# RWKV on one NeuronCore: zeros behind the first norms, an order edge on the scaling of y, and gate stores from another queue

## The chip, the core and the metric

The kernel runs on one core of a Trainium2 chip. The metric is the device time of one execution in microseconds (us). The kernel before took 1004.63 us, the median of three runs (1004.32 to 1005.11). A core has a matrix engine, TensorE (PE; its weight loads are listed as PEld), three engines for element-wise work, VectorE (DVE), ScalarE (ACT) and GpSimd (POOL), and SyncE (SP), which here only issues DMA transfers. ACT and POOL can issue transfers too. Each engine works through its own list of instructions in order, and waits for the others by semaphores.

## The reference

One layer of a hybrid decoder on 512 prompt tokens and 8 x 8 sampled tokens (576 columns in all), all in float32. RWKV-7 time mixing and a paged differential attention read the same normalised input; sigmoid gates mix their outputs; then comes an MLP. The parts that matter here:

```python
def rwkv7_scan(S0, r, w, k, v, a, b):
    def step(S, inp):
        r_t, w_t, k_t, v_t, a_t, b_t = inp
        sa = jnp.einsum('bhij,bhj->bhi', S, a_t)
        S = S * w_t[:, :, None, :] + sa[..., None] * b_t[:, :, None, :] + v_t[..., None] * k_t[:, :, None, :]
        return S, jnp.einsum('bhij,bhj->bhi', S, r_t)
    S, ys = lax.scan(step, S0.astype(jnp.float32), xs)

def rwkv7_branch(Pr, S0, lp):
    ...
    kk = kk / jnp.maximum(jnp.linalg.norm(kk, axis=-1, keepdims=True), 1e-12)
    ...
    S, y = rwkv7_scan(S0, hs(r), hs(decay), hs(k), hs(v), -kk, kk * hs(a))
    mean = jnp.mean(y, axis=-1, keepdims=True)
    var = jnp.mean(jnp.square(y - mean), axis=-1, keepdims=True)
    y = (y - mean) * lax.rsqrt(var + GN_EPS) * lp['ln_x_w'] ... + lp['ln_x_b'] ...
    ...

def layer_forward(x, prev_row, S0, attend, lam_init, lp):
    ...
    gate_a = jax.nn.sigmoid(P[..., off2:off2 + D_MODEL])
    gate_b = jax.nn.sigmoid(P[..., off2 + D_MODEL:off2 + 2 * D_MODEL])
    m = gate_a * (o_a @ lp['w_br_a']) + gate_b * (o_b @ lp['w_br_b'])
```

## The kernel before

Activations lie with channels on the 128 partitions and the 576 tokens along the free axis. A product with a weight matrix is a *stream*: weights are loaded as `raw` tiles by SP, split into a rounded part `hi` (ACT) and a rest `lo` (DVE), and PE runs three matmuls for each block of weights (`xh,hi`, `xl,hi`, `xh,lo`) over two halves of the columns. The result lands in a bank (`ps_g`, `ps_z`), from which DVE evacuates it.

The eight heads of RWKV are worked on as four pairs of heads, `hp` 0 to 3, and these two at a time (`pr` 0 and 1). For each `hp` the generator `rwkv(hp)` runs in stages:

- The first stage (lines 751 to 840) makes the norms of k: `sq`, its sums `pn` on PE, `nr` on DVE, the power -0.5 on POOL (L760), and `nb`, the norm spread out over 64 columns, by a copy on POOL (L763). PE transposes `nb` to `pk` and `pks`, and DVE multiplies k by them (`sq` again, the unit key). Decays come by a scan on DVE (`cum`) and exponentials on ACT (`pe`, `pinv`, `u`). Then DVE writes the tiles KB and ST, PE multiplies them (`pA`), and DVE evacuates them to ABR and ST. One half of each ST is cleared by POOL (L818).
- The second stage puts v into SVU (transposes `pV`), KB into KBt (`pK`), and loads the sampled sequences' state `s0` (L859, SP). `pI` on PE multiplies ST and that state. POOL copies an identity into SVU (L871) and clears a part of it (L872).
- The third inverts the 32x32 blocks (`pW`, `pZ`, matmuls of 32x32 tiles) and writes TT; POOL clears two parts of TT (L923, L924).
- The fourth updates the state: `pF` on PE, whose input `vm` comes from POOL; two operations on DVE (`s<-s,pF`, the addition, and `s<-s,pc`, the scaling); and a store by POOL's queue (L941). The tile of `hp` + 2's state uses the buffer of `hp`'s.
- The last ones, behind the recurrence, normalise y over 64 columns: `mean`, the square, `var`, a power on POOL, the scaling `tt(y, y, b9(var), MUL)` on DVE (L958), transposes `pTy`, and the products with the gate of RWKV, `pg`.

`chain(pr)` is the recurrence over nine chunks of 64 tokens: small matmuls `pch` and `pY` (64x64 tiles), each waiting for a copy on ACT or DVE. Between them the scheduler puts the gate matmuls: `gate(g)` for 16 blocks of output channels streams w_in (`ps_g`), scales each half (`gg`, DVE), applies tanh (ACT), and stores the result in `gt_d` in device memory (L452), from where it is read back at the merge.

What stands where on each engine is set by the scheduler: it takes the program's order, the priorities that `prio` sets, and order edges, `tc.issue_after(x)`, which keep an instruction behind instruction x in the list. `ring["mm"]` is the last matmul or transpose so far, `take(n)` lets the streams that are waiting advance by n steps.

Of the kernel before, what the change touches and what calls it, by code (L numbers as in the profile page):

```python
# [15 lines left out]
P = 128  # L16
# [20 lines left out]
C_ID, C_OB, C_M, C_MS, C_LM, C_I32, C_HS, C_SEL, C_MB, C_CM, C_END = (  # L37
    0, 128, 256, 384, 512, 672, 704, 706, 738, 746, 748)
# [3 lines left out]
def tile_hybrid_step(ctx, tc, xT, xsT, ktab, vtab, s0T, ptab, w_in, vecs, w2a2, g2, lamv,  # L42
                     w_bra, w_brb, w_out, w_up, w_down, cst, bias_p, bias_s,
                     yT, kTo, vTo, Sp, Ss, sh):
    nc = tc.nc
    PE, VE, AE, GE = nc.tensor, nc.vector, nc.scalar, nc.gpsimd
# [8 lines left out]
    ring = {"job": 0}  # L55

    def act(out, in_, func=AF.Copy, **kw):
        ring["act"] = AE.activation(out=out, in_=in_, func=func, **kw)  # L58

    def tt(out, a, b, op, eng=None):  # L60
        ins = (eng or VE).tensor_tensor(out=out, in0=a, in1=b, op=op)  # L61
        if eng is None:
            ring["tt"] = ins

    def stt(out, a, s, b, op0, op1):
        VE.scalar_tensor_tensor(out=out, in0=a, scalar=s, in1=b, op0=op0, op1=op1)
# [4 lines left out]
    def mm(out, lhsT, rhs, start=True, stop=True):  # L71
        ring["mm"] = PE.matmul(out=out, lhsT=lhsT, rhs=rhs, start=start, stop=stop)  # L72
        return ring["mm"]
# [17 lines left out]
    MUL, ADD, SUB, MAX = ALU.mult, ALU.add, ALU.subtract, ALU.max  # L91
# [12 lines left out]
    def tbank(name):  # L104
        return psc.tile([P, 512], F32, tag="t", name=name)
# [6 lines left out]
    c = const.tile([P, C_END], F32, name="cst_sb")  # L112
# [103 lines left out]
    def take(n):  # L216

        while waiting and n:
            if next(waiting[0], None) is None:
                waiting.pop(0)  # L220
            else:
                n -= 1
# [42 lines left out]
    gt_d = tc.dram_tile([2 * KT, P, NT], F32, name="gt_d")  # L265
# [178 lines left out]
    def gate(g):  # L444

        gg = gs.tile([P, NT], F32, tag="gg", name=f"gg{g}")

        def ev(ps, t0, n):
            tt(gg[:, t0:t0 + n], ps, R1[:, t0:t0 + n], MUL)
            act(gg[:, t0:t0 + n], gg[:, t0:t0 + n], AF.Tanh, scale=0.5)  # L450
        yield from stream(w_in[26 + g], KT, xh, xl, HALF, ev, f"g{g}")
        nc.sync.dma_start(out=gt_d[g], in_=gg)  # L452

    def ob_halves():

# [209 lines left out]
    for h in range(HB):  # L665
        if h:
            qkv(h)
        for cc in range(2):
            GE.tensor_copy(
                out=qbd[64 * cc:64 * cc + 64, :, h, 8 * cc:8 * cc + 8],  # L670
                in_=qT[64 * cc:64 * cc + 64, h, NPR:].rearrange("p (b q) -> p b q", b=NB))
# [47 lines left out]
    def ch(a):  # L719
        return a.rearrange("p (c t) -> p c t", t=64)  # L720

    def m3(ap_, n):
        q, w = ap_.shape
        return ap_.rearrange("p (o w) -> p o w", o=1).broadcast_to([q, n, w])
# [17 lines left out]
    def rwkv(hp):  # L742
# [5 lines left out]
        def tmp(tag, bufs=1):  # L748
            return rt.tile([P, NT], F32, tag="T", name=f"{tag}_{hp}", bufs=6)


        sq = tmp("sq")
        act(sq, k, AF.Square, scale=v(V_KK + hp))
        pn = bank(f"pn{hp}")
        for t, o in enumerate(toks):
            mm(pn[:, 2 * t:2 * t + 2], sq[:, o:o + P], c[:, C_HS:C_HS + 2])
        (fill if hp != 2 else take)(8)
        nr = stat.tile([P, 10], F32, tag="nr", name=f"nr{hp}")
# [1 line left out]
        GE.tensor_tensor(out=nr, in0=nr, in1=mhalf[:, :10], op=ALU.pow)  # L760

        nb = rt.tile([P, 5, P], F32, tag="G", name=f"nb{hp}", bufs=3)
        GE.tensor_copy(out=nb.rearrange("p t (a d) -> p (t a) d", a=2),  # L763
                       in_=nr.rearrange("p (a o) -> p a o", o=1).broadcast_to([P, 10, 64]))
        u = tmp("u")
        aa = tmp("aa")
        for t0, n in HALF:
# [46 lines left out]
        for par, rows in halves:  # L814
            stt(KB[rows, :, par], ch(aa)[rows], 0.5, ch(pinv)[rows], MUL, MUL)
            tt(KB[rows, :, 1 - par], ch(k2)[rows], ch(pinv)[rows], MUL)
            st = rb_.tile([P, NCH, 2, 64], F32, tag=f"ST{par}", name=f"ST{par}_{hp}")
            GE.memset(st[64 - 64 * par:128 - 64 * par], 0.0)  # L818
            stt(st[rows, :, 0], ch(kk)[rows], -1.0, ch(pm)[rows], MUL, MUL)
            tt(st[rows, :, 1], ch(r)[rows], ch(pe)[rows], MUL)  # L820
            ST.append(st)
# [4 lines left out]
        for par in range(2):  # L826
            rows = slice(64 * par, 64 * par + 64)
# [14 lines left out]
        SVU = own["SVU"][:, :, e]  # L842
# [23 lines left out]
        for par in range(2):  # L866
            rows = slice(64 * par, 64 * par + 64)
            for a in range(2):
                act(ST[par][rows, 8, a].rearrange("p (b t) -> p b t", b=NB),
                    pI[rows, 0:P].rearrange("p (b a t) -> p b a t", b=NB, a=2)[:, :, a])  # L870
            GE.tensor_copy(out=SVU[rows, 8, par], in_=c[rows, C_ID + 64 * par:C_ID + 64 * par + 64])  # L871
            GE.memset(SVU[rows, 0, par], 0.0)  # L872

        yield

# [10 lines left out]
        def blocks(ps, lhs, rhs, n):  # L886
            for ci in range(n):
                for g in range(4):
                    gs = slice(32 * g, 32 * g + 32)
                    last = mm(ps[gs, ci * 32:ci * 32 + 32], lhs[gs, ci], rhs[gs, ci])  # L890
            with tc.issue_after(last.ins):
                take(9)
            return ps[:, :n * 32].rearrange("p (c s) -> p c s", c=n)
# [3 lines left out]
        for l in range(1, 5):  # L897

            n = NCH if l < 3 else 8
            DM = rt.tile([P, NCH, 32], F32, tag="DM", name=f"DM{hp}_{l}")  # L900
            tt(DM[:, :n], DT[:, :n], m3(c[:, C_LM + 32 * l:C_LM + 32 * l + 32], n), MUL)
            W = rt.tile([P, NCH, 32], F32, tag="W", name=f"W{hp}_{l}")
            act(W[:, :n], blocks(tbank(f"pW{hp}{l}"), DM, X, n))
            tt(X[:, :n], X[:, :n], blocks(tbank(f"pZ{hp}{l}"), Y, W, n), ADD)
            VE.transpose(out=Y[:, :n], in_=X[:, :n])
        TT = rb_.tile([P, NCH, 64], F32, tag="TT", name=f"TT{hp}")
        pW = tbank(f"pWc{hp}")
# [11 lines left out]
        for b0, b1 in quads:  # L919
            act(TT[b0, :8, 32:64], pC[b0, :256].rearrange("p (c s) -> p c s", c=8))  # L920
            act(TT[b0, :, 0:32], Y[b0])
            act(TT[b1, :, 32:64], Y[b1])
            GE.memset(TT[b0, 8:, 32:64], 0.0)  # L923
            GE.memset(TT[b1, :, 0:32], 0.0)  # L924

        own[e] = ST, KBt, TT, ABR, pc
        yield
# [16 lines left out]
        y = own["y"][:, e]  # L944
# [4 lines left out]
        b9 = lambda a: a.rearrange("p (c o) -> p c o", o=1).broadcast_to([P, NCH, 64])  # L949
# [3 lines left out]
        var = stat.tile([P, NCH], F32, tag="var", name=f"var{hp}")  # L953
# [1 line left out]
        rpow(var, var, 1.0 / 64, 64e-5)  # L955

        yield
        tt(y, y, b9(var), MUL)  # L958
        oa = rt.tile([P, NT], F32, tag="G", bufs=3, name=f"oa{hp}")
        if hp >= 2:  # L960
            half_rows(hp)
# [79 lines left out]


    gens = [rwkv(hp) for hp in range(4)]

    def run(*stages):
        for hp in stages:
            while Pt[8 + hp] is None:
                take(2)
            next(gens[hp], None)

    waiting += zs(2) + zs(3) + [gate(g) for g in range(KT, 2 * KT)]
    ga = [gate(g) for g in range(KT)]
    waiting += ga[:5]
    run(0, 0)
# [33 lines left out]
    for d in range(KT):  # L1088
        g = []
        for i in range(2):  # L1090
            gg = rt.tile([P, NT], F32, tag="T", name=f"g{i}_{d}", bufs=6)
# [32 lines left out]
    for i, d in enumerate((0, 4, 1, 5, 2, 6, 3, 7)):  # L1124
# [31 lines left out]
        for j, (t0, n) in enumerate(HALF):  # L1156
            o = acc[:, t0:t0 + n]
# [142 lines left out]
    rows = []  # L1300
    for d, n in enumerate((None, "t1", "b11", "t2", "b21", "t3", "b22", "t4")):
        if n:
            t = fp.tile([P, 2, 4, 288], F32R, tag=f"h_{n}", name=f"w3_{d}", bufs=1)
            t = t.rearrange("p i k t -> p (i k t)")
# [179 lines left out]
```

## Time and profile before

| | us |
|---|---|
| median of three runs (lowest, highest) | 1004.63 (1004.32, 1005.11) |
| the profiled execution's own time | 1006.88 |
| its span | 1005.1 |
| PE busy in the span | 975.1 (97%) |
| DVE busy | 688.9 (69%) |
| ACT busy | 497.0 (49%) |
| POOL busy | 87.5 (9%) |
| mean granted clock of PE | 0.993 |

The profile is of one execution. The span is from the first to the last instruction that it recorded. Rows of a timeline have the start in us, the duration, the engine, the line of the kernel, the operation, output<-inputs with their shapes, and the number of instructions in the row; in square brackets stand the engine's idle time before and what ended it. A row with several instructions lasts from the start of the first to the end of the last. Matmuls overlap, so that their starts tell how fast PE goes on. `SPq`, `ACTq` and `POOLq` are the queues on which an engine issues transfers. The names in the timeline leave the buffers' numbers out.

### The profile page before, as it was taken

To read this page: it belongs to the slowest core of one execution; us is meant where nothing else is said; L and a number is where in the kernel's file an instruction comes from. 1 tells how busy PE (TensorE), PEld (TensorE's weight loads), DVE (VectorE), ACT (ScalarE), POOL (GpSimd) and SP (SyncE) were. 2 spreads that over 40 slices of the span, in tenths; PEclk is the share of its full clock that TensorE was granted. 3 is DMA by queue.
4 is the path that set the end of the run, shared out by engine and by line. 5 is a ranking of instruction groups with operands and counts; after the bars stand their busy time and mean duration, and the time that the engine had idled before them with its cause. 6 is when DMAs were issued, how large, how long until landed. Compare 5 with 4: busy or idle time off the path is not lost.

```text
span 1005.1 us, 24415 instructions
## 1 busy us (share of the span) xinstructions
PE 975.1 (97%) x10012; PEld 919.4 (91%) x10012; DVE 688.9 (69%) x1459; ACT 497.0 (49%) x1094; POOL 87.5 (9%) x171
## 2 busy tenths in 40 slices
PE   9999999899999998999989999999999999999996
PEld 9999998898887887988779999999999999999996
DVE  6698566864946679444579898966666666666644
ACT  6576455354435355453334666644444444444732
POOL 2511001301010340000210000000000000000001
PEclk9999999999989999999999999999999999999999
DMA  7422673211111234323357642222222222221402
GB/s 266 136 70 83 205 223 114 61 64 45 43 59 45 69 106 152 104 81 113 103 182 225 206 140 86 83 95 85 88 92 85 85 84 85 84 87 41 135 3 95
DMA packets 50833, 105.75 MB, mean 105 GB/s; under 512 B 6066, under 2 KB 8114, under 8 KB 50594
## 3 DMA queue, kind: packets, MB, share of 16 engines
q1 hardware_dynamic: 47442, 96.95, 30.4%
q0 software_dynamic: 1648, 5.35, 1.5%
q8 instruction: 79, 1.29, 0.5%
q10 hardware_dynamic: 1632, 1.89, 0.5%
q14 instruction: 32, 0.26, 0.1%
HBM read 89.38 MB, written 14.78 MB: 104 GB/s over the span
## 4 chain that ended last, share of the span: by engine, by line
PE 83%; DVE 6%; ACT 4%; issue 3%; DMA 2%; POOL 1%; SPq 0%; DVEq 0%; ACTq 0%; POOLq 0%
PE ps_dn L72 20%; PE ps_g L72 8%; PE ps_z L72 8%; PE ua L1220 5%; PE ux L1220 5%; PE ps_wo L72 4%; PE ps_k L72 3%; PE uc L1220 3%; PE ub L1220 3%; PE ud L1220 2%; PE ps_bra L72 2%; PE ps_q L72 2%; PE pch L72 2%; PE ps_brb L72 2%; PE ps_v L72 2%
## 5 line engine op out<-in xcount | busy, mean ns | idle before, releaser
L72 PE MATMUL ps_dn<-q,hi_dn 128*128 128x288 f32 x768 | 154.7, 296 | 0.0
L72 PEld LDWEIGHTS ps_dn<-q,hi_dn 128*128 128x128 f32 x768 | 122.7, 188 | 1.4
L72 PE MATMUL ps_dn<-q,lo_dn 128*128 128x288 f32 x384 | 113.2, 295 | 0.0
L72 PE MATMUL ps_g<-xl,hi_g 128*128 128x288 f32 x256 | 79.7, 311 | 0.0
L72 PE MATMUL ps_g<-xh,hi_g 128*128 128x288 f32 x256 | 79.0, 309 | 0.0
L72 PE MATMUL ps_g<-xh,lo_g 128*128 128x288 f32 x256 | 79.0, 309 | 0.0
L72 PEld LDWEIGHTS ps_dn<-q,lo_dn 128*128 128x128 f32 x384 | 72.0, 188 | 0.0
L72 PE MATMUL ps_z<-xh,lo_z 128*128 128x288 f32 (+1 forms) x224 | 68.9, 308 | 0.0
L72 PE MATMUL ps_z<-xh,hi_z 128*128 128x288 f32 (+1 forms) x224 | 67.6, 302 | 0.0
L72 PE MATMUL ps_z<-xl,hi_z 128*128 128x288 f32 (+1 forms) x224 | 66.8, 298 | 0.0
L61 DVE TENSOR_TENSOR ya<-ya,ps_dn 128x288 f32<-128x288 f32 x96 | 43.2, 451 | 29.4 <-PE ps_dn L72 29.4
L58 ACT ACTIVATE hi_dn<-raw_dn 128x512 fp32r<-128x512 f32 x48 | 30.1, 628 | 57.0 <-PE ps_dn L72 57.0
L1220 PE MATMUL ua<-h_b,hi 128*128 128x288 f32 x256 | 53.2, 298 | 0.0
L1220 PE MATMUL ux<-h_t,hi 128*128 128x288 f32 x256 | 52.3, 296 | 0.0
L58 ACT ACTIVATE c<-c 128x288 f32<-128x288 f32 x112 | 48.4, 439 | 7.4 <-DVE c L61 5.8
L72 PEld LDWEIGHTS ps_g<-xh,hi_g 128*128 128x128 f32 x256 | 48.7, 190 | 3.1 <-issue 1.8
L72 PEld LDWEIGHTS ps_g<-xl,hi_g 128*128 128x128 f32 x256 | 48.6, 190 | 1.9
L72 PEld LDWEIGHTS ps_g<-xh,lo_g 128*128 128x128 f32 x256 | 48.6, 190 | 1.6 <-DVE lo_g L61 0.2
L58 ACT ACTIVATE hi<-a 128x1024 fp32r<-128x1024 f32 (+1 forms) x32 | 27.1, 846 | 42.0 <-PE ps_dn L72 34.2
L72 PE MATMUL ps_dn<-q,w 128*128 128x320 f32 (+1 forms) x336 | 46.3, 297 | 0.0
L61 DVE TENSOR_TENSOR lo<-s,hi 128x1024 fp32r<-128x1024 f32 x32 | 39.2, 1224 | 10.1 <-ACT hi L58 10.0
L72 PEld LDWEIGHTS ps_dn<-q,w 128*128 128x128 f32 x336 | 45.3, 190 | 0.1
(395 smaller groups left out, 2802.2 us busy)
## 6 DMA issues: line engine op xcount, KB each, us to landing
a<-in_w_up_dram SPq DMA_DIRECT2D x32, 512.0 KB, 3.4
raw_dn<-in_w_down_dram SPq DMA_DIRECT2D x64, 256.0 KB, 2.8
raw_g<-in_w_in_dram SPq DMA_DIRECT2D x32, 256.0 KB, 3.1
raw_z<-in_w_in_dram SPq DMA_DIRECT2D x28, 256.0 KB, 3.1
gt_d<-gg SPq DMA_DIRECT2D x16, 288.0 KB, 2.4
g<-gt_d SPq DMA_DIRECT2D x16, 288.0 KB, 3.6
kp<-in_ktab_dram SPq DMA_DIRECT2D x16, 256.0 KB, 4.5
vp<-in_vtab_dram SPq DMA_DIRECT2D x16, 256.0 KB, 3.8
```

Of the source, the lines that this page charges most:

```text
L58: ring["act"] = AE.activation(out=out, in_=in_, func=func, **kw)
L61: ins = (eng or VE).tensor_tensor(out=out, in0=a, in1=b, op=op)
L72: ring["mm"] = PE.matmul(out=out, lhsT=lhsT, rhs=rhs, start=start, stop=stop)
L1220: ring["mm"] = PE.matmul(out=ps[:, :288], lhsT=l[:, k], rhs=hb[blk][:, h, k], start=start and i == 0, stop=i == 11, skip_group_check=skip)
```

## The change

Three edits:

1. `clear(a)` takes the place of POOL's memsets of ST, SVU and TT. For `hp` 0 it keeps the memset behind the copy to `nb` (an order edge); for the others it is the plain memset. The copy of the identity into SVU stands behind `nb` for every `hp`.
2. The scaling of y gets an order edge behind a matmul: for `hp` 0 and 1 behind `ring["mid"]`, which is set at the fourth step of the block inversion of the `hp` that ran it last, and for 2 and 3 behind the last matmul so far.
3. The store of each gate block is issued on ACT's queue and no longer on SP's.

```diff
@@ gate(g)
         yield from stream(w_in[26 + g], KT, xh, xl, HALF, ev, f"g{g}")
-        nc.sync.dma_start(out=gt_d[g], in_=gg)
+        nc.scalar.dma_start(out=gt_d[g], in_=gg)
@@ rwkv(hp)
+        def clear(a):
+            if hp:
+                GE.memset(a, 0.0)
+            else:
+                with tc.issue_after(ring["nb"].ins):
+                    GE.memset(a, 0.0)
...
-        GE.tensor_copy(out=nb.rearrange("p t (a d) -> p (t a) d", a=2),
+        ring["nb"] = GE.tensor_copy(out=nb.rearrange("p t (a d) -> p (t a) d", a=2),
...
-            GE.memset(st[64 - 64 * par:128 - 64 * par], 0.0)
+            clear(st[64 - 64 * par:128 - 64 * par])
...
-            GE.tensor_copy(out=SVU[rows, 8, par], in_=c[rows, C_ID + 64 * par:C_ID + 64 * par + 64])
-            GE.memset(SVU[rows, 0, par], 0.0)
+            with tc.issue_after(ring["nb"].ins):
+                GE.tensor_copy(out=SVU[rows, 8, par], in_=c[rows, C_ID + 64 * par:C_ID + 64 * par + 64])
+            clear(SVU[rows, 0, par])
...
             tt(X[:, :n], X[:, :n], blocks(tbank(f"pZ{hp}{l}"), Y, W, n), ADD)
+            if l == 3:
+                ring["mid"] = ring["mm"]
             VE.transpose(out=Y[:, :n], in_=X[:, :n])
...
-            GE.memset(TT[b0, 8:, 32:64], 0.0)
-            GE.memset(TT[b1, :, 0:32], 0.0)
+            clear(TT[b0, 8:, 32:64])
+            clear(TT[b1, :, 0:32])
...
-        tt(y, y, b9(var), MUL)
+        with tc.issue_after((ring["mid"] if hp < 2 else ring["mm"]).ins):
+            tt(y, y, b9(var), MUL)
```

The first place is POOL's list at the first norms, before:

```order
L711 DMA ob_d<-obs 128x4x64
L818 MEMSET ST_0_2814 64x1152
L818 MEMSET ST_0_2820 64x1152
L760 TENSOR_TENSOR nr_2749<-nr_2749,mhalf 128x10
L871 COPY SVU_2861<-cst_sb 64x64
L872 MEMSET SVU_2861 64x64
L763 COPY nb_2752<-nr_2749 128x640
L871 COPY SVU_2861<-cst_sb 64x64
```

and of the changed kernel:

```order
L712 DMA ob_d<-obs 128x4x64
L755 MEMSET SVU_2861 64x64 x2
L769 TENSOR_TENSOR nr_2749<-nr_2749,mhalf 128x10
L772 COPY nb_2752<-nr_2749 128x640
L758 MEMSET ST_0_2814 64x1152
L758 MEMSET ST_0_2820 64x1152
L881 COPY SVU_2861<-cst_sb 64x64
L758 MEMSET SVU_2861 64x64
```

The memsets of ST and the copies into SVU now stand behind `nb`; two small memsets of SVU, which belong to another `hp`, stand ahead of the power.

The second place is PE's list in the first recurrence, at its second chunk (`pch` and `pY` of that chunk, `ps_g` of a gate, `pk` of `hp` 1), before:

```order
L76 MATMUL pk_4920<-cst_sb,nb_4884 128x128
L72 MATMUL pch_4602<-SVU_2861,ST_0_2814 64x64
L72 MATMUL pch_4602<-SVU_2861,ST_0_2820 64x64
L72 MATMUL pch_4602<-SVU_2861,ST_1_3829 64x64
L72 MATMUL pch_4602<-SVU_2861,ST_1_3835 64x64
L72 MATMUL pY_4603<-SVU_2861,ST_0_2814 64x64
L72 MATMUL pY_4603<-SVU_2861,ST_0_2820 64x64
L72 MATMUL pY_4603<-SVU_2861,ST_1_3829 64x64
L72 MATMUL pY_4603<-SVU_2861,ST_1_3835 64x64
```

and of the changed kernel:

```order
L72 MATMUL pch_4602<-SVU_2861,ST_0_2814 64x64
L72 MATMUL pY_4603<-SVU_2861,ST_0_2814 64x64
L72 MATMUL ps_g_0_4512<-xl,hi_g_1_4508 128x288
L72 MATMUL ps_g_0_4512<-xh,lo_g_1_4509 128x288
L72 MATMUL pch_4602<-SVU_2861,ST_0_2820 64x64
L72 MATMUL pch_4602<-SVU_2861,ST_1_3829 64x64
L72 MATMUL pY_4603<-SVU_2861,ST_0_2820 64x64
L72 MATMUL pY_4603<-SVU_2861,ST_1_3829 64x64
L72 MATMUL pch_4602<-SVU_2861,ST_1_3835 64x64
L72 MATMUL pY_4603<-SVU_2861,ST_1_3835 64x64
```

The eight small matmuls stood together; now two gate matmuls stand between them, and in other places some that stood apart stand together. Over the whole list PE changes between full 128x128 matmuls and small tiles 262 times before and 274 times now.

The third place is DVE's list where the states of `hp` 0 and 1 are finished (`s_0`, `s_1`), before:

```order
L61 TENSOR_TENSOR s_0_2891<-s_0_2891,pF_4992 128x512
L61 TENSOR_TENSOR s_1_3905<-s_1_3905,pF_5002 128x512
L61 TENSOR_TENSOR s_0_2891<-s_0_2891,pc_2782 128x512
L61 TENSOR_TENSOR lo_g_1_5259<-raw_g_4_5252,hi_g_1_5258 128x512
L61 TENSOR_TENSOR s_1_3905<-s_1_3905,pc_3797 128x512
L61 TENSOR_TENSOR gg_5181<-ps_g_1_5195,R_108 128x288
L61 TENSOR_TENSOR lo_g_0_5407<-raw_g_0_5402,hi_g_0_5406 128x512
L61 TENSOR_TENSOR Y_5614<-DT_5609,cst_sb 128x288
```

and of the changed kernel:

```order
L61 TENSOR_TENSOR s_0_2891<-s_0_2891,pF_4992 128x512
L61 TENSOR_TENSOR s_1_3905<-s_1_3905,pF_5002 128x512
L61 TENSOR_TENSOR gg_5181<-ps_g_1_5195,R_108 128x288
L61 TENSOR_TENSOR lo_g_0_5407<-raw_g_0_5402,hi_g_0_5406 128x512
L61 TENSOR_TENSOR s_0_2891<-s_0_2891,pc_2782 128x512
L61 TENSOR_TENSOR s_1_3905<-s_1_3905,pc_3797 128x512
L61 TENSOR_TENSOR Y_5614<-DT_5609,cst_sb 128x288
```

One evacuation of a gate and one split of weights now stand ahead of the scaling. On PE the second `pF` has three gate matmuls between it and the first, where it had six, and 46 instead of 58 gate matmuls lie between the first `pF` and `pI`, with thirty `pW` more.

The list of POOL differs by edit 1, and one memset of ST for `hp` 3 moves as well; those of PE, DVE, ACT and SP by edit 3 alone. With edit 2 alone every list reads as before.

More of the change, by code (lines that the diff above doesn't have):

```diff
@@ L762, in rwkv @@
         nb = rt.tile([P, 5, P], F32, tag="G", name=f"nb{hp}", bufs=3)
-        GE.tensor_copy(out=nb.rearrange("p t (a d) -> p (t a) d", a=2),
-                       in_=nr.rearrange("p (a o) -> p a o", o=1).broadcast_to([P, 10, 64]))
+        ring["nb"] = GE.tensor_copy(out=nb.rearrange("p t (a d) -> p (t a) d", a=2),
+                                    in_=nr.rearrange("p (a o) -> p a o", o=1).broadcast_to([P, 10, 64]))
         u = tmp("u")
```

## The prediction

> **What bounds the kernel now.** I read the head of the page first, then the list of what TensorE (PE) waited for, then timelines of the places that the change touches. The first fence has the span and the busy shares, and from the list of waits the rows that come up below; their columns are total us, times, longest us.
>
> ```profile
> span 1005.1 us, 24415 instructions
> PE 975.1 (97%) x10012; PEld 919.4 (91%) x10012; DVE 688.9 (69%) x1459; ACT 497.0 (49%) x1094; POOL 87.5 (9%) x171
> ...
> PE pk L76 <- POOL nb L763: 2.7, 1, 2.7
> ...
> PE pTy L76 <- DVE y L61: 1.2, 1, 1.2
> ...
> PE pI L72 <- DMA s<-in_s0T_dram: 0.7, 1, 0.7
> ...
> PE pch L72 <- ACT SVU L58: 0.5, 1, 0.5
> ...
> PE pF L72 <- POOL vm L61: 0.3, 1, 0.3
> ```
>
> PE is busy for 975.1 of 1005.1 us, so only 30 us of the span are idle time of PE. A change gains what it takes from those 30 us and loses what it adds to them or to PE's own work. The longest single wait, 2.7 us, is for `nb` in the first norms, where the change begins. SyncE (SP), ScalarE (ACT) and GpSimd (POOL) count only where PE ends up waiting for them.
>
> **The zeros on GpSimd.** The timeline round the first norms, one piece for each of POOL, PE and DVE, with a row that sums a later stretch:
>
> ```profile
> 177.01 2.16 POOL L818 MEMSET ST<- 64x1152 f32 x2
> 179.14 2.18 POOL L760 TENSOR_TENSOR nr<-nr,mhalf 128x10 f32<-128x10 f32 x1
> ...
> 181.47 0.14 POOL L872 MEMSET SVU<- 64x64 f32 x1
> 181.56 0.71 POOL L763 COPY nb<-nr 128x640 f32<-128x640 f32 x1
> ...
> 179.37 0.30 PE L72 MATMUL ps_z<-xh,lo_z 128*128 128x296 f32 x1
> 182.32 0.66 PE L76 MATMUL pk<-cst_sb,nb 128*128 128x128 f32 x4 [2.66 <-POOL nb L763]
> ...
> 175.79 0.16 DVE L69 TENSOR_SCALAR nr<-pn 128x10 f32<-128x10 f32 x1
> ...
> 180.79 0.43 DVE L61 TENSOR_TENSOR Z<-ps_z,R 128x288 f32<-128x288 f32 x1
> 183.02 0.75 DVE L66 SCALAR_TENSOR_TENSOR sq<-P,vec,pk 128x512 f32<-128x512 f32 x1 [1.79 <-PE pk L76]
> ...
> 190.00:200.00 10.00, 9.79 (x72) 9.10 (x70) 9.80 (x17) 1.27 (x2) 0.00 (x0) 1.00 0.21 59
> ```
>
> The input of the power `nr` is there at 175.95 (175.79 + 0.16), but POOL clears the two halves of ST until 179.17 before it starts. In the new order two small clears of SVU (0.14 each) stand in that place; both wait only for things of long before. The power then starts at 177.01 + 0.3 = 177.3 and ends at 179.5, and `nb` follows at once and ends at 180.2 instead of 182.27. PE has nothing else until `pk` and ended its matmul at 179.67, so its wait shrinks from 2.66 to some 0.6 us: -2.1. Who is late next is VectorE (DVE): it is busy with Z until 181.22, so `sq` starts there instead of at 183.02: -1.8. Behind `sq` DVE is busy in 9.80 of the 10 us from 190 on, and PE waits for that work at `pbn`, so I take what DVE gains, **-1.8 us**. The bounds are -2.1 and 0: zero if the later part of that stretch ends on something else than DVE. The clears of ST now come behind `nb` and end at 180.2 + 2.16 = 182.4; what reads ST comes behind the work that DVE only begins with `sq`, so this work hides them. Were they needed at once, PE would lose up to those 2.2 us again.
>
> **The scaling of y.** The new wait names a matmul, and an order edge behind it; the instruction on DVE keeps its neighbours, and no row on any engine moves for this edit alone. It costs and gains **0**. Had it moved the scaling behind more work, PE's 1.2 us wait of `pTy` for y is where it would show.
>
> **The gate stores.** Sixteen DMA issues leave SP's queue and enter ACT's. These are the issues of the stores now, of a store on ACT, and two rows on waiting:
>
> ```profile
> L452 SPq DMA_DIRECT2D gt_d<-gg x16: 319/326/331, 287.7 to 498.5; - x16
> ...
> L1366 ACTq DMA_DIRECT2D out_yT_dram<-ya x4: 378/388/407, 983.2 to 1001.3; - x4
> ...
> SPq L452 <- ACT gg L58: 34.4, 14, 5.3
> ...
> ACT hi_g L58 <- PE ps_g L72: 20.6, 16, 2.8
> ```
>
> On ACT they cost 16 x 0.39 = 6.2 us, on an engine that is busy for 49%. SP is rid of 34.4 us of waiting ahead of the weight loads queued behind a store. But that was not on the path: the split of gate weights on ACT (`hi_g`) waits for PE to let go of a buffer, 16 times, not for a load. So the move itself gives and takes about 0; the upper bound is one issue of 0.39 on the way mean, square, y, `pTy` of the last pair, where a store stands ahead of the square: 0 to +0.4, and I take +0.1.
>
> What does cost is that the order of the other engines changes with it. First, the recurrence (`pch`, `pY`) is cut into smaller groups among the gate matmuls. A stretch of PE's timeline shows the price:
>
> ```profile
> 309.48 0.29 PE L72 MATMUL ps_g<-xl,hi_g 128*128 128x288 f32 x1
> 309.61 0.29 PE L72 MATMUL ps_g<-xh,lo_g 128*128 128x288 f32 x1
> 309.83 0.45 PE L72 MATMUL pch<-SVU,KBt 128*64 128x64 f32 x8
> 310.21 0.45 PE L72 MATMUL pY<-SVU,ABR 64*64 64x64 f32 x8
> 310.59 0.40 PE L72 MATMUL ps_g<-xh,hi_g 128*128 128x288 f32 x1
> 310.83 0.30 PE L72 MATMUL ps_g<-xl,hi_g 128*128 128x288 f32 x1
> ```
>
> Gate matmuls start 0.13 apart (309.48, 309.61); from the last of them to the first small one it is 0.22, and the first gate matmul behind the small ones holds its place for 0.24 before the next. Each switch so costs about 0.1 us. Counted over the two orders PE switches 262 times before and 274 times now: 12 x 0.1 = **+1.2** (bounds 0.5 and 1.5). Against it, a matmul of the recurrence that stands later waits less for ACT and DVE; the list of waits has 0.5 us for `pch` behind SVU as its largest: **-0.4** (bounds -0.9 and 0).
>
> Second, the load of the next pair's state. It overwrites the buffer of the first pair's state, so it waits for that state's store, which waits for two additions and two scalings on DVE. The rows in order of time, the load from the chain of waits, and the landing times of the store (2.4/3.2/4.5) and of the load:
>
> ```profile
> 354.71 0.40 PE L72 MATMUL ps_g<-xh,hi_g 128*128 128x288 f32 x1
> 354.81 0.69 DVE L61 TENSOR_TENSOR s<-s,pF 128x512 f32<-128x512 f32 x1 [0.91 <-PE pF L72]
> 355.42 0.69 DVE L61 TENSOR_TENSOR s<-s,pc 128x512 f32<-128x512 f32 x1
> 356.40 0.57 POOL L941 DMA_DIRECT2D out_Ss_dram<-s  x1 [1.28 <-DVE s L61]
> 357.55 0.45 DVE L61 TENSOR_TENSOR gg<-ps_g,R 128x288 f32<-128x288 f32 x1
> 357.98 0.69 DVE L61 TENSOR_TENSOR lo_g<-raw_g,hi_g 128x512 fp32r<-128x512 f32 x1
> 358.59 0.45 DVE L61 TENSOR_TENSOR Y<-DT,cst_sb 128x288 f32<-128x288 f32 x1
> ...
> 359.44 4.86 DMA s<-in_s0T_dram
> ...
> 364.44 1.11 PE L72 MATMUL pI<-ST,s 64*64 64x16 f32 x32 [0.66 <-DMA s<-in_s0T_dram]
> ...
> DMA to landing us min/median/max: 2.4/3.2/4.5
> ...
> DMA to landing us min/median/max: 3.6/4.0/4.9
> ```
>
> In the new order the evacuation `gg<-ps_g` and the split `lo_g` stand between the additions and the scaling. The evacuation needs the nine gate matmuls behind the second `pF`: they start with the second addition, 9 x 0.13 = 1.2 us. Then come 0.43 (357.55 to 357.98) and 0.61 (to 358.59). The scaling starts at 354.81 + 1.3 + 0.43 + 0.61 = 357.15 instead of 355.42, 1.7 us later, and store and load with it. PE, however, gets to `pI` sooner after `pF`: 12 gate matmuls fewer lie between (-1.6), thirty small `pW` more (+0.6), and the second `pF` has three gate matmuls ahead of it instead of six, so that its wait for `vm` (0.3 now) grows by some 0.4. That makes 0.6 less. The wait at `pI` becomes 0.66 + 1.7 + 0.6 = 3.0 us, or 2.1 if the load lands in its median of 4.0 instead of 4.86. With the 0.4 at `pF` the place costs between 1.9 and 2.7; I take **+2.2**, and keep 0 below (a load that lands in 3.6 behind a store that lands in 2.4, with PE held up elsewhere) and 3.2 above.
>
> **Sum:** -1.8 + 0 + 0.1 + 1.2 - 0.4 + 2.2 = +1.3 us. The profiled execution took 1006.88 us for its span of 1005.1; the median of the runs is 1004.63, 2.25 below it. I carry the difference over: 1008.2 for a profiled execution, **1005.9 us** as a median. A measurement here can tell about 0.2% (2.0 us) from no change, and +1.3 is less.
>
> **Rivals.** *The orders are free and only the zeros count.* The wait at `pI` stays at 0.66, if the store's landing and not DVE's place in line decides, and the switches hide in waits. For it: the load took 4.86 where its median is 4.0. Against it: the store is issued right behind the scaling. Then -1.8 and little else, 1002.8; with the other -0.4, 1002.4.
>
> *A half clock behind the new wait.* These are two windows of the span (length, then busy time of PE, PEld, DVE, ACT and POOL, then the granted clock):
>
> ```profile
> 508.85:512.26 3.41, 1.55 (x8) 1.09 (x9) 1.75 (x4) 1.83 (x6) 1.58 (x1) 1.00 0.76 227
> 512.26:515.68 3.42, 3.42 (x14) 3.20 (x13) 3.10 (x6) 0.42 (x2) 0.22 (x1) 0.50 0.39 115
> ```
>
> After a window of 3.41 us in which PE worked 1.55 us, the next is granted half the clock. A 3 us wait at `pI`, followed by small matmuls, could make such a window. The price is at most half of one window, 1.7 us; since PE also waits there I put 1.5 on top of the sum: 1007.4, slower than before by 2.8. It decides from the point where the wait exceeds about half a window inside one of them. Against it: the 2.66 us wait at 179.67 had full clock behind it. The Trainium skill ("TensorE: Matmul & The Clock Gate", Part 1, "What's actually happening") speaks of a free-running window of 3413 ns and of half clock after a window that was idle. By that rule a wait of 3.0 us, shorter than a window, would cost no clock; the row of 1.55 us of work does not agree with it.
>
> *The zeros' gain is given back.* DVE's early start at 181.2 ends in a wait for ACT's exponentials or for weights before 205, and the rest stands: 0 + 0.1 + 0.8 + 2.2 = +3.1, 1007.7.
>
> **How the numbers follow.** The sum as worked out 0.45, within 1004.0 to 1007.2 by the bounds of its terms; the free orders 0.25; the half clock 0.2; the gain given back 0.1. Faster by over 2.0 us (below 1002.6) happens in some two thirds of the second case and hardly in the first: 0.19. Slower by over 2.0 (above 1006.6) has the half clock, the gain given back and about a tenth of the sum's own case: 0.34. Within: 0.47. The range runs from 1002.5, where the free orders begin, to 1008.6, the half clock with the upper bound at `pI`.
>
> **What would show it.** Right: `pk` waits some 0.6 us for `nb` and `sq` starts 1.8 earlier; the longest wait of PE is then `pI` for the state's load, 2 to 3 us; the gate stores' issues on ACT take 0.39 and SP's list lacks them; the y waits are as before. Wrong: `pI` waits under 1 us, or `pbn` takes up what `pk` lost, or a second window of half clock stands near 366, or PE's work between 285 and 350 has not grown by about 1 us.

## The result and the profile after

The changed kernel takes 1013.95 us, the median of five runs (1011.52 to 1015.28), against 1004.89 us for the kernel before in the same comparison (1004.32 to 1005.94, five runs). The ratio is 1.0079 with a 95% interval of 1.0066 to 1.0092: about 8 us slower by the ratio and 9.1 by the medians, where 1.3 us were forecast and 1008.6 us was the end of the range. (The ratio is worked out from the runs of both kernels and is not the quotient of their medians.) The profiled execution took 1011.52 us, the fastest of the five, and that of the kernel before, 1006.88, lies above its median. The two profiles are thus only 4.6 us apart: they show where time goes, and not all of its amount.

The head of the page and the list of PE's waits of the changed kernel answer to the first rows of the prediction:

```profile
span 1009.7 us, 24407 instructions
PE 978.4 (97%) x10012; PEld 921.4 (91%) x10012; DVE 692.0 (69%) x1459; ACT 497.3 (49%) x1094; POOL 88.8 (9%) x171
...
PE pA L72 <- DVE ST L61: 2.6, 1, 2.6
PE pI L72 <- DMA s<-in_s0T_dram: 2.1, 1, 2.1
...
PE pk L76 <- POOL nb L772: 1.4, 1, 1.4
...
PE pTy L76 <- DVE y L61: 1.1, 1, 1.1
```

The wait at `pk` fell from 2.7 to 1.4 us and the wait at `pI` grew from 0.7 to 2.1, both as the prediction said in kind. The longest wait is one that it did not have: `pA` waits 2.6 us for DVE to write ST, at 350.88. The timeline of POOL, DVE and PE ahead of that wait shows where it comes from:

```profile
342.81 2.17 POOL L755 MEMSET ST<- 64x1152 f32 x2
344.96 3.04 POOL L61 TENSOR_TENSOR vm<-SVU,cst_sb 128x512 f32<-128x512 f32 x3
348.06 2.16 POOL L755 MEMSET ST<- 64x1152 f32 x2
...
343.79 0.74 DVE L61 TENSOR_TENSOR ST<-P,pe 64x576 f32<-64x576 f32 x1
344.56 4.05 DVE L66 SCALAR_TENSOR_TENSOR ST<-sq,u 64x576 f32<-64x576 f32 x1
348.54 0.75 DVE L61 TENSOR_TENSOR ST<-P,pe 64x576 f32<-64x576 f32 x1
...
350.88 1.13 PE L72 MATMUL pA<-ST,KB 128*128 128x128 f32 x8 [2.59 <-DVE ST L61]
```

The same rows of POOL and DVE in the kernel before:

```profile
342.05 3.27 POOL L818 MEMSET ST<- 64x1152 f32 x3
345.41 3.55 POOL L61 TENSOR_TENSOR vm<-SVU,cst_sb 128x512 f32<-128x512 f32 x3
...
344.61 0.76 DVE L66 SCALAR_TENSOR_TENSOR ST<-sq,u 64x576 f32<-64x576 f32 x1
345.29 0.75 DVE L61 TENSOR_TENSOR ST<-P,pe 64x576 f32<-64x576 f32 x1
```

An operation on DVE that took 0.76 us there (at 344.61) lasts 4.05 us in the changed kernel, from 344.56 to 348.61. It ends 0.6 us after POOL's three `vm` products, which read SBUF, have ended at 348.0. While POOL only clears ST (342.81 to 344.98), DVE's operation at 343.79 takes its usual 0.74. The loss does not show as idle time ahead of the instruction but as its duration: it has started and does not get on. The Trainium skill ("SBUF — State Buffer", "SBUF: two separate sides") states that DVE and GpSimd share one port pair under an exclusive lock, that an operation on DVE with two SBUF inputs contends for it with a GpSimd operation that reads SBUF, and that whichever starts first holds it for its whole instruction while the other is blocked. The row agrees with the blocking and not with who comes first: DVE's operation began at 344.56, 0.4 us ahead of POOL's first product at 344.96.

Behind the two long waits stand windows of half clock. The columns are the length, the busy times of PE, PEld, DVE, ACT and POOL, then the granted clock:

```profile
348.69:352.10 3.41, 1.23 (x10) 1.26 (x11) 3.29 (x6) 0.26 (x1) 2.31 (x6) 1.00 0.00 0
352.10:355.51 3.41, 3.41 (x18) 3.41 (x17) 2.56 (x6) 1.07 (x3) 0.00 (x0) 0.50 0.00 0
369.17:372.58 3.41, 2.44 (x44) 2.44 (x45) 0.09 (x1) 0.33 (x2) 0.00 (x0) 1.00 0.37 119
372.58:375.99 3.41, 3.41 (x12) 2.91 (x12) 2.31 (x6) 2.72 (x6) 3.05 (x4) 0.50 0.23 71
```

PE is busy through both half windows, so each costs about 1.7 us of its work (half of 3.41, an estimate). In exchange the profile of after has one half window near 277 where that of before had two, and none near 512, so that both have three up to 990 us. The mean granted clock is 0.9916 over the 97 runs of before beside the experiments and 0.9904 over the five of after, a difference worth 0.0012 x 1004 = 1.2 us, which five runs hardly tell from none (single runs go from 0.986 to 0.994). Over the 17 runs of the three kernels with both long waits (the change, the stores alone, the swapped writes) it is 0.9898, worth 1.8 us.

### The profile page after: what moved, and what is told of

It reads as the page before. It is cut to its first block, busy times and chain, and to the rows that moved or that the text cites. A ratio compares the mean times of both kernels' runs of the same rounds, so it can differ in the third digit from the quotient of the medians.

```text
span 1009.7 us, 24407 instructions
## 1 busy us (share of the span) xinstructions
PE 978.4 (97%) x10012; PEld 921.4 (91%) x10012; DVE 692.0 (69%) x1459; ACT 497.3 (49%) x1094; POOL 88.8 (9%) x171
## 4 chain that ended last, share of the span: by engine, by line
PE 84%; DVE 6%; ACT 4%; issue 2%; DMA 2%; POOL 2%; SPq 0%; DVEq 0%; POOLq 0%; ACTq 0%
PE ps_dn L72 20%; PE ps_g L72 9%; PE ps_z L72 8%; PE ua L1234 5%; PE ux L1234 5%; PE ps_wo L72 4%; PE ps_k L72 3%; PE uc L1234 3%; PE ub L1234 3%; PE ps_bra L72 2%; PE ud L1234 2%; PE pch L72 2%; PE ps_q L72 2%; PE ps_v L72 2%; PE ps_brb L72 2%
```

## The experiments

Medians are of 12 runs where nothing else is said. The kernel before was run beside every group and took 1004.58 to 1004.96.

| kernel | median us | ratio to before (95%) |
|---|---|---|
| the change (5 runs) | 1013.95 | 1.0079 (1.0066 to 1.0092) |
| zeros alone | 1003.25 | 0.9979 (0.9966 to 0.9992) |
| stores alone (6 runs) | 1014.29 | 1.0086 (1.0063 to 1.0109) |
| change, one clearing moved back | 1008.63 | 1.0033 (1.0017 to 1.0049) |
| before, that clearing moved | 1005.39 | 1.0006 (0.9991 to 1.0021) |
| change, ST writes swapped (6 runs) | 1012.83 | 1.0072 (1.0055 to 1.0090) |
| change, scalings first | 1010.39 | 1.0051 (1.0034 to 1.0067) |
| change, both put right | 1007.14 | 1.0023 (1.0010 to 1.0037) |
| the same, y really later | 1006.82 | 1.0007 (0.9993 to 1.0021) |
| zeros, 11 stores on ACT, order kept | 1003.18 | 0.9988 (0.9976 to 1.0000) |
| zeros, `nb` on ACT | 1003.14 | 0.9980 (0.9967 to 0.9992) |
| zeros, y really later (11 runs) | 1001.06 | 0.9960 (0.9947 to 0.9972) |
| zeros, y later, `nb` on ACT (6 runs) | 998.06 | 0.9944 (0.9923 to 0.9966) |

### Which edit carries the loss

Edit 1 alone (`clear` and the edge behind `nb`; gate stores on SP, the scaling of y as before):

> Edit 1 alone: the zeros behind nb, the gate stores on SP as before. Theory 'port': the nb copy (0.71 us with VectorE at rest) takes about 1.5 us because VectorE's scan runs beside it, so pk waits some 1.4 us instead of 2.66 and the kernel gains 1.0 to 1.2 us: 1003.8. Theory 'as predicted': nb takes 0.71, pk waits 0.6, gain 1.8: 1003.1. Theory 'all of the loss comes with the zeros': 1010 or more. Either of the first two leaves PE's list of waits otherwise as before (pI 0.7, no pA).

It gives 1003.25 us, ratio 0.9979: a gain of 1.6 us in the medians and 2.1 by the ratio. `pk` waits 1.4 us, as the first theory had it; the time cannot tell the first two theories apart. Edit 3 alone:

```diff
-        nc.sync.dma_start(out=gt_d[g], in_=gg)
+        nc.scalar.dma_start(out=gt_d[g], in_=gg)
```

> Edit 3 alone: the gate stores from ACT's queue, zeros as before. Theory 'C carries all': the 4 us ST operation on VectorE near 345, the pA wait of 2.6 and the pI wait of 2 are there as in the changed kernel, and the time is the changed kernel's plus the 1 us that the zeros gain: about 1014 to 1015. Theory 'the two edits only hurt together': 1005 to 1008, without the 4 us operation.

1014.29 us. The 4 us operation is there (4.11 us at 347.01), and so are the waits at `pA` (2.6) and `pI` (2.2). All of the loss comes with the stores, and the zeros only win.

### One clearing on GpSimd

With the stores on ACT the scheduler moves one row of POOL: the clearing of ST0 of `hp` 3 stands behind the three `vm` products and no longer ahead of them. This run puts that row back, and nothing else differs on any engine:

```diff
-            clear(st[64 - 64 * par:128 - 64 * par])
+            with prio(tc.cur_priority - 350 if hp == 3 and par == 0 else tc.cur_priority):
+                clear(st[64 - 64 * par:128 - 64 * par])
```

> The changed kernel with one instruction moved back on GpSimd: the clearing of ST0 of hp 3 stands ahead of the three vm products again, as before. Theory 'port': the ST operation on VectorE takes 0.75 instead of 4.05, the pA wait of 2.59 goes, and with it the half clock window at 352; the pI wait of 2.1 stays: 4 us faster than the changed kernel, about 1009 to 1010. Theory 'order and switches': PE, VectorE and ACT keep their lists, so nothing changes: 1013 to 1014. Theory 'state load': pI stays, and only 1 us or less is gained.

1008.63 us, 5.3 us faster than the change (4.6 by the ratios, 1.0079 and 1.0033). The same rows of POOL and DVE as above, and the first wait of PE's list:

```profile
342.40 3.27 POOL L755 MEMSET ST<- 64x1152 f32 x3
345.76 3.05 POOL L61 TENSOR_TENSOR vm<-SVU,cst_sb 128x512 f32<-128x512 f32 x3
...
344.15 0.76 DVE L66 SCALAR_TENSOR_TENSOR ST<-sq,u 64x576 f32<-64x576 f32 x1
344.83 0.75 DVE L61 TENSOR_TENSOR ST<-P,pe 64x576 f32<-64x576 f32 x1
```

```profile
PE pI L72 <- DMA s<-in_s0T_dram: 2.4, 1, 2.4
```

The third clearing keeps POOL busy until 345.67, DVE's two operations end at 345.58, and only then do the products read. The `pA` wait is gone from the list. So the row cost the `pA` wait of 2.6 us and another 2 to 2.7; the half window behind that wait, some 1.7, is gone from this profile too.

The reverse, the kernel before with that one row moved behind the products (by order edges between POOL's instructions; all other lists as before):

```diff
-            GE.memset(st[64 - 64 * par:128 - 64 * par], 0.0)
+            with (tc.issue_after(ring["vm"].ins) if hp == 3 else ExitStack()):
+                ring["vm"] = GE.memset(st[64 - 64 * par:128 - 64 * par], 0.0)
...
+            if hp == 1 and par == 0:
+                ring["vm"] = vi
```

> The kernel before with that one instruction moved: the clearing of ST0 of hp 3 behind the three vm products, all else as before, on every engine. Theory 'port': the vm products now start near 344.2 and an ST operation on VectorE that starts at 344.6 lasts until they end near 347.3; pA waits some 2 us and a half clock window may follow: 1007 to 1009. Theory 'order and switches' and 'state load': no change, 1004.9.

1005.39 us, ratio 1.0006: no difference. The theory expected 2 to 4 us here, and was wrong. POOL and DVE in that run:

```profile
343.00 4.07 POOL L935 TENSOR_TENSOR vm<-SVU,cst_sb 128x512 f32<-128x512 f32 x3 [0.53 <-DVE SVU L1015]
...
342.88 0.76 DVE L66 SCALAR_TENSOR_TENSOR ST<-sq,u 64x576 f32<-64x576 f32 x1
343.56 1.60 DVE L61 TENSOR_TENSOR ST<-P,pe 64x576 f32<-64x576 f32 x1
```

Here the products wait for DVE's copy into SVU, and DVE's operation, which in this order stands right behind that copy, is already reading when the first product comes. Now both take turns: the three products take 4.07 us instead of 3.04, and DVE's second operation 1.60 instead of 0.75. That delay of 0.85 us costs PE 0.23 at `pA`. So the moved row alone does not do it; it takes the new order of the other engines as well. On DVE that order has the copy into SVU and a write of ST ahead of the operation that is held up, but no run changed that by itself.

Is it the form of the operation? The two writes of ST1 of `hp` 2 in the other order, in the changed kernel:

```diff
+            if hp == 2 and par == 1:
+                tt(st[rows, :, 1], ch(r)[rows], ch(pe)[rows], MUL)
+                stt(st[rows, :, 0], ch(kk)[rows], -1.0, ch(pm)[rows], MUL, MUL)
```

> The changed kernel with the two operations on VectorE that write ST1 of hp 2 in the other order, the two-input product first and the three-operand one second. Theory 'GpSimd keeps the port over instructions that follow each other': whichever stands first lasts 4 us; time as the changed kernel, 1013 to 1014. Theory 'the three-operand form alone waits for all three': the first lasts 1 to 1.6 us and the second no longer either: pA waits under 1 us, 1009 to 1011.

1012.83 us, about as the change. DVE's rows:

```profile
343.36 4.82 DVE L61 TENSOR_TENSOR ST<-P,pe 64x576 f32<-64x576 f32 x2
348.10 0.75 DVE L66 SCALAR_TENSOR_TENSOR ST<-sq,u 64x576 f32<-64x576 f32 x1
```

Now it is the plain product that lasts 4.05 us (the second of the two in the first row) and the three-operand one that takes 0.75. Whichever stands there waits for all three products.

### The state's load

The two scalings ahead of the evacuation and the split:

```diff
-        tt(sn, sn, pc[:, 8:16].rearrange("p (b o) -> p b o", o=1).broadcast_to([P, NB, 64]), MUL)
+        with prio(FEED - 1 if hp < 2 else tc.cur_priority):
+            tt(sn, sn, pc[:, 8:16].rearrange("p (b o) -> p b o", o=1).broadcast_to([P, NB, 64]), MUL)
```

> The changed kernel with the two scalings of the state right behind the two additions on VectorE (the clearing of ST0 stays where the change put it). Theory 'port and state load': the pA wait of 2.6 and its half clock window stay, the pI wait falls from 2.1 to under 0.7 and the half clock window behind it goes: 3 to 4 us faster than the changed kernel, 1010 to 1011. Theory 'only the port': pI falls but the time does not, 1013 to 1014.

1010.39 us, 3.6 faster than the change. The wait for the load is gone. But the scheduler also moves other rows of PE, DVE and ACT, and a wait of 1.9 us of `ps_g`, near 381, has taken its place, so this figure is not the price of the load alone. Both repairs together:

> The changed kernel with both put right: the clearing of ST0 ahead of the vm products, the scalings right behind the additions. Theory 'port and state load': neither a wait of 2 us at pA nor at pI is left; what remains against the zeros alone (1003.25) is the 12 more switches of PE, about 1 us: 1004 to 1006. Theory 'the stores on ACT cost by themselves' (6 us of issues): 1008 or more.

1007.14 us, 6.8 faster than the change and 3.9 slower than the zeros alone, where about 1 was expected. From the run before it this one differs by the same single row of POOL, which so has a second price: 3.2 us (1010.39 to 1007.14; 2.8 by the ratios). PE's first wait and DVE's row behind it:

```profile
PE ps_g L72 <- DVE pc L791: 2.0, 1, 2.0
```

```profile
377.49 0.76 DVE L61 TENSOR_TENSOR y<-y,var 128x576 f32<-128x576 f32 x1 [1.91 <-POOL var L243]
```

DVE waits 1.91 us for POOL's power ahead of the scaling of y, with an evacuation of a gate queued behind it for which PE waits. That is what edit 2 means to prevent, and does not, since its edge names a matmul. This run gives the scaling an edge between two instructions of DVE:

```diff
         tt(cum, cum, u, SUB)
+        ring["cum"] = ring["tt"]
...
-        with tc.issue_after((ring["mid"] if hp < 2 else ring["mm"]).ins):
+        with (tc.issue_after(ring["cum"].ins) if hp < 2 else ExitStack()):
             tt(y, y, b9(var), MUL)
```

> The changed kernel with clearing and scalings put right, and the scaling of y for hp 0 and 1 really later on VectorE: behind the subtraction of cum of hp 3, by an order edge between two instructions of VectorE (in the change the edge names a matmul and moves nothing). Theory 'what is late next': the 1.95 us wait of PE near 379, behind VectorE's wait for the power of y, goes and its half clock window too: 1003 to 1004.5, level with the zeros alone. Theory 'the stores on ACT cost by themselves': it stays at 1006 to 1007.

1006.82 us in the median; by the ratio of 1.0007 some 1.5 us faster than without it, so the two readings disagree on the size. The wait near 379 is gone, and `pA` now waits 2.4 us for KB at 388.03. Neither expected time came: each repair of the new order uncovers a wait behind it. Beside its own partner, the zeros with the same later scaling and the stores on SP (1001.06 below), this kernel is still 5.8 us slower, 4.7 by the ratios. The stores cost 10.7 us against the zeros alone (1003.25 to 1013.95); the two repairs take back some half to two thirds of that, and the rest stays.

### The queue without the order

Each store taken singly, eleven can be moved to ACT so that the lists of PE, DVE and POOL stay row for row those of the zeros alone:

```diff
+        (nc.scalar if g in (8, 14, 0, 1, 2, 3, 4, 7, 11, 13, 15) else nc.sync).dma_start(out=gt_d[g], in_=gg)
```

> The zeros alone, and eleven of the sixteen gate stores (gates 0 to 4, 7, 8, 11, 13, 14 and 15) from ACT's queue; these are the ones that leave the lists of PE, VectorE and GpSimd as they are, so that only the queue changes. Theory 'the order, not the queue': level with the zeros alone, 1002.8 to 1004. Theory 'issues on ACT cost': up to 11 x 0.35 = 3.9 us more, 1005 to 1007.

1003.18 us, against 1003.25 without them; the ratios, 0.9988 and 0.9979, lie within each other's intervals. The row of their issues:

```profile
L453 ACTq DMA_DIRECT2D gt_d<-gg x11: 326/327/345, 285.8 to 497.0; - x11
```

Eleven issues of 0.327 us on ACT cost nothing that can be measured, where the second theory had up to 3.9 us. So for these eleven the cost is the order and not the queue; the other five could not be tried without a new order.

### The copy to `nb`

In the changed kernel the copy takes 1.57 us. POOL, DVE and PE there:

```profile
177.61 1.99 POOL L769 TENSOR_TENSOR nr<-nr,mhalf 128x10 f32<-128x10 f32 x1
179.66 1.57 POOL L772 COPY nb<-nr 128x640 f32<-128x640 f32 x1
...
179.36 1.36 DVE L786 TENSOR_TENSOR_SCAN cum<-reset,u 128x576 f32<-128x576 f32 x1
...
181.29 0.66 PE L76 MATMUL pk<-cst_sb,nb 128*128 128x128 f32 x4 [1.44 <-POOL nb L772]
```

Now that it starts earlier it stands beside DVE's scan, which reads two inputs from SBUF, until 180.72; before it stood beside nothing and took 0.71. The same copy for other `hp` in the kernel before takes 1.25 us beside a split on DVE, which has two inputs in SBUF (245.65), and 0.72 beside a reduction with one (369.15). To test this, the copy of the first norms goes to ACT, behind `aa`, and the zeros behind the power:

```diff
+        if hp:
+            ring["nb"] = GE.tensor_copy(out=nbo, in_=nri)
...
+        if hp == 0:
+            with tc.issue_after(ring["act"].ins):
+                act(nbo, nri)
```

> The zeros alone, and the nb copy of the first norms made by ACT instead of GpSimd, with the power as before. Theory 'port': the copy takes about 0.75 us on ACT beside the scan, pk waits some 0.7 us instead of 1.4, and 0.5 to 0.8 us are gained on the zeros alone: 1002.6, which is the gain of 1.8 that was forecast. Theory 'the copy is slow for another reason' (the spread read of nr): it takes 1.5 us on ACT too, 1003.3.

```profile
178.81 0.74 ACT L58 ACTIVATE nb<-nr 128x640 f32<-128x640 f32 x1 [0.30 <-POOL nr L769]
...
178.55 1.36 DVE L791 TENSOR_TENSOR_SCAN cum<-reset,u 128x576 f32<-128x576 f32 x1
...
179.60 0.66 PE L76 MATMUL pk<-cst_sb,nb 128*128 128x128 f32 x4 [0.30 <-ACT nb L58]
```

Beside the same scan the copy takes 0.74 us on ACT, and PE waits 0.30. With the rows at 245.65 and 369.15 this makes DVE's reads of two inputs the cause of the 1.57. The median, however, is 1003.14, no better than the zeros alone. The run also moves other rows of PE and DVE, its profile has two half windows at 363 to 370 that the zeros alone lack, and intervals of 1.3 us to either side could hide the 1.1 us that PE no longer waits here; what became of them is open.

### A version that beats both

The really later scaling of y, without the stores:

> The zeros alone with that same later scaling of y, the stores on SP. In the zeros alone VectorE does not wait for the power of y, so theory 'what is late next' gives at most what the pbn wait of 1.8 us behind the scaling holds: 1001.5 to 1003.3. Theory 'any new order costs': over 1004.

1001.06 us, ratio 0.9960, just beyond the good end of what was expected. The edge moves one operation on DVE and the scheduler then many rows of PE and DVE, so that the 2 us against the zeros alone are those of a whole new order. With the copy on ACT as well:

> The zeros, the really later scaling of y, and the nb copy of the first norms on ACT, stores on SP: the best of the parts together. Theory 'port': as the zeros with the later y (1001.06) or up to 0.8 faster, 1000.2 to 1001.1, pk waits 0.3. Theory 'any new order costs': over 1002.

998.06 us, ratio 0.9944 (0.9923 to 0.9966): 6.5 us better than the kernel before beside it (1004.58) and 16 better than the change. Expected were at most 0.8 us over the run before, and the medians have 3.0; the intervals overlap, and where more would come from was not followed up. Edits 1 and 2 gain when the edge of edit 2 acts.

## Why the prediction was wrong

The direction of the sum was right and its size was not: +1.3 us forecast, +9.1 in the medians. By its own steps:

- **The zeros, -1.8.** The rows came out smaller. The step took `nb` with the 0.71 us of its old place; in its new place beside the scan it takes 1.57. PE's wait fell to 1.44 and not to 0.6, and `sq` starts 6.0 us behind `nr` on DVE (175.98 to 181.98) where it was 7.2 before (175.79 to 183.02): 1.2 us gained and not 1.8.

```profile
181.98 0.75 DVE L66 SCALAR_TENSOR_TENSOR sq<-P,vec,pk 128x512 f32<-128x512 f32 x1 [0.91 <-PE pk L76]
```

  The time of the zeros alone, 1.6 us in the medians and 2.1 by the ratio (0.8 to 3.4), fits both. On ACT, where the copy takes 0.74, the wait fell to 0.30, but no more time came of it that can be measured.
- **The scaling of y, 0.** As forecast: `pTy` waits 1.1 us where it waited 1.2. The prediction said the edge moves nothing; it did not ask what a real one would give, which is some 2 us with all the rows that move behind it (1003.25 to 1001.06).
- **The issues on ACT, +0.1.** Right: 0.327 us each where 0.39 was taken, and eleven of them cost nothing.
- **The state's load, +2.2.** Right in mechanism and nearly in size. The chain of waits of the changed kernel, in order of time (start, duration, what):

```profile
361.59 0.69 DVE lo_g L61
362.28 0.61 DVE s L61
362.89 0.29 issue
363.18 4.21 DMA out_Ss_dram<-s
...
367.53 2.48 DMA s<-in_s0T_dram
```

  Evacuation, split, scaling, store, load follow each other as the step said. The wait came to 2.1 us, the lower of the two values given. The scaling came 1.9 us later behind the addition, where the step had 1.7. Store and load took 4.21 and 2.48 us, with 0.15 between them. Before, the store took 2.41 (356.40 to 358.81), the load then stood 0.63 us in SP's queue behind a gate store and a weight load, which the step overlooked, and took 4.86. From issue to landing that is 6.8 us against 7.9, which is why the lower value came: the landing times, and not the reasoning, decided between the two. The 0.4 at `pF` did not come: the wait of 0.3 in the list stands at 500.89 before and at 507.09 after, in the second pair, and the step had put it at the first. And sixty `pW` moved ahead of `pI` (the row at 367.34, 0.72 us), not thirty; at the step's price of 0.6 this changes little.
- **The step that failed: the sum over the reordered engines.** It priced the new order with three terms (switches, waits of the recurrence, the load) and put POOL's list, of which the section on the change says that one memset of ST moves, at nothing without a reason. That row and the new order of DVE's writes of ST together put three reads of POOL over one operation of DVE: 4.05 us instead of 0.75, 2.6 us of PE's wait, and 5.3 us of time when it is taken back (3.2 where the scalings were put right first).
- **The switches, +1.2 with -0.4.** Too small, as the profiles show it. These are the stretches from `pI` of `hp` 1 to `pI` of `hp` 2 in the kernel before, the change, the zeros alone and the change with both put right (columns as in the windows above):

```profile
275.41:364.44 89.03, 87.03 (x1356) 73.41 (x1356) 56.77 (x138) 38.69 (x97) 15.81 (x26) 0.96 0.22 70
274.53:370.14 95.61, 89.99 (x1415) 75.17 (x1416) 60.38 (x138) 38.79 (x97) 14.99 (x24) 0.96 0.20 64
273.64:362.35 88.71, 87.16 (x1356) 73.56 (x1356) 56.70 (x138) 38.76 (x97) 15.47 (x24) 0.96 0.22 70
274.30:363.49 89.19, 88.17 (x1355) 73.00 (x1355) 56.08 (x137) 38.80 (x97) 15.46 (x24) 0.98 0.22 69
```

  The first three have two half windows in the stretch and the last has one. From before to after PE is busy for 3.0 us more, 0.7 of which are the sixty `pW`. Of the last two, which work through the same matmuls without a long wait (the counts differ by one at the edges), the repaired one is busy for 1.0 us more with one half window less; at 1.7 us for that window its work has grown by 2.7. So the new order costs PE 2 to 3 us of its own work in this stretch alone, where +0.8 was forecast for the whole kernel. Whether it is the switches (90 instead of 81 here from before to after, 0.9 us at the price of the step) or something else in the order, no run tested.
- **The half clock, a rival with 0.2.** It happened at the place named, behind `pI` at 372.58, and behind the `pA` wait too. Its price of 1.5 fits one window, but other windows went, so the net is the 1 to 2 us above. The condition was wrong: PE waited for 0.97 us in the window before, and not for over half of it. The rule of the Trainium skill ("TensorE: Matmul & The Clock Gate", Part 1, "What's actually happening") asks for an idle window; here PE had worked 2.44 of 3.41 us, nearly all of it in matmuls of 16 and 2 columns (`pI`, `pn`). The measurement decides.
- **The gain given back, and the free orders.** Neither: the zeros' gain is there alone, and the order is not free.
- **The bounds of the sum, 1004.0 to 1007.2.** They do not follow from those of its terms: the narrow ones (1.9 to 2.7 for the load) with the zeros at -2.1 to 0 give 1004.0 to 1009.2, and the wide ones (0 to 3.2) 1002.1 to 1009.7. The measured time lies outside these too.

What the repairs leave was not tested: with both in place and y later the kernel is still 5.8 us behind the zeros with y later. The profiles show where some of it may lie: PE's 2 to 3 us of work above, and the `pA` wait of 2.4 us for KB with a half window behind it. A version of the stores on ACT with the old order could be had for eleven of them only.

## What to carry to other kernels

When a scheduler sets the order, compare the lists of every engine, the least busy too, and for each row that moves ask what now runs beside it; with GpSimd and VectorE, whether both read SBUF. One clearing on an engine busy for 9% cost 3 to 5 us here, more than the whole sum that was forecast. A duration taken from the trace holds for the neighbours that it had there. An order edge acts only between instructions whose order it can change: to move an operation on one engine, name an instruction of that engine.

## What the runs showed of the hardware

- Three reads of POOL in a row can hold up one operation of DVE for all of them (4.0 to 4.1 us, in four kernels: the change, the stores alone, the swapped writes and the scalings first). DVE's operation had then begun some 0.4 us ahead of the first read (344.56 and 344.96), while POOL was still clearing. In the kernel before DVE's product began 0.12 us ahead (345.29 and 345.41), kept its 0.75, and POOL's three took 3.55 instead of 3.04. With the one row moved the two took turns (4.07 us for the three products, 1.60 for DVE's second operation). What decides between these was not settled.
- Clearing on POOL does not hold DVE up: 0.74 to 0.76 us beside it, as without.
- The same contention lengthens POOL's side: the copy to `nb` takes 0.71 alone, 0.72 beside a reduction with one input, 1.25 beside a split and 1.57 beside a scan.
